# Two products held behind the weight split, and another order for the first transfers, in a hybrid recurrent and attention block

## The chip, the cores and the metric

The kernel runs on one core of a Trainium2 chip. The metric is the device time of one execution in microseconds (us); less is better. A profiled execution has a time of its own, and its trace gives start and length of every instruction on TensorE (PE), VectorE (DVE), ScalarE (ACT), GpSimd (POOL) and the queue of SyncE (SP), which issues all transfers here.

## The reference, cut to what matters

One layer of a residual block, in fp32, on one sequence of 512 positions with 2048 features:

```python
mod = silu(c) @ ada_w + ada_b             # six vectors of 2048: shift and scale (here SH1, SC1), gates, ...
h   = rms_norm(x) * (1 + scale) + shift   # adaLN modulation
p   = h @ w_in                            # recurrent x (1024) | recurrent y (1024) | 8 heads of q, k, v | forget logits
rec = rglru(conv4(p_x), gates) * gelu(p_y)            # width-4 causal convolution, then a scan along the positions
att = softmax(rms_norm(q) @ rms_norm(k).T + cum_logf) @ v   # 8 heads of 128, causal, 128-query blocks
x   = x + gate1 * (concat(rms_norm(rec), rms_norm(att)) @ w_out)
x   = x + gate2 * swiglu(modulate(rms_norm(x)))       # up projection, down projection
```

## The kernel before, in words

**Numbers.** Every fp32 product with a weight is made of three matmuls on rounded halves: both operands are split into a high part (an ACT copy to fp32r) and a low part (a DVE subtraction), and PE sums high x high, low x high and high x low. `wsplit` (L196) does this for a weight tile: whi on ACT, wlo on DVE. `tail_lo` is the list of the DVE subtractions issued so far, so `tail_lo[-1]` is the split of the newest weight tile at that place of the program.

**Stages in time.** Features lie on the 128 partitions, positions along a row (tiles of 128x512). From about 12 to 103 us `w1`: the first 1024 input columns, 16 steps (kt) of 24 matmuls into 8 PSUM banks. To 150 us `yr0`, from 150 to 185 us the first half of `h0`, to 503 us the heads `h1` to `h7`, each a projection (`tm_group`) into whose steps the attention of the head before, a pair of recurrent blocks, bias sums and adaLN products are hung as hooks. Then `yr1`, the output projection, the up projection and the down projection.

**The step of w1.** Before x is normed, the scale A of a feature must be known. For each kt `ada_fast(SC1, kt)` (L151) loads two 128x1024 tiles of the adaLN weight, `ada` and `adf`, and DVE multiplies each with silu(c), kept on all partitions in `c_b` and summed along the row (L159). L340 and L342 make A of the two sums, of `bg` (1 + a slice of `vec`, the table of all small vectors) and of a column of `vec`. ACT writes hph = x·A rounded (L345), DVE hpl (L346); ACT and DVE split the weights w1r into w1h and w1l (L352, L353); ACT squares x for the norm (L288). `c_b` comes of the input row `crow`: half is broadcast by a transfer, half by PE (cps), and ACT applies silu to both. `SH1` products run the same way under `yr0`, followed by `make_h`: x·A·rstd_x (L382), hh and hl (L384, L385), where rstd_x is the norm's factor, made at about 105 to 110 us.

**Attention and recurrence in the heads.** `attention()` gives a list of steps: `stats` (squares, sums, POOL's power), `norm` (L487: q and k times their factor), `qk_t` (transposes), `score` (L515 on PE, then on DVE the negated row maximum nm, L520, and later bt scaled by its sum, L524), `pt_` (transposes pt on PE, evacuated by ACT to pT, L534) and `pv` (L542 on PE into po). `rec_pair()` gives the recurrent steps: `fetch`, `conv` (L623: xrl times rstd_x on DVE, then the bias on ACT, L624, and the taps), `gates`, the scan. `ada_some` issues products of the other adaLN vectors (L149), always behind `tail_lo[-1]`; `bias_in` (L601) sums what the shift adds to the projections; `forget` makes the cumulative log-forget sums, which go to DRAM as `ct` and come back as `cb`.

**What sets the order.** The program is traced in source order and then scheduled per engine by priority. `tc.high_priority(offset)` moves an instruction forward; `with tc.issue_after(ins)` keeps what is issued inside it behind `ins` on the engine. Each engine then runs its list strictly in that order. All transfers go out on SP's queue in SP's order.

Of the kernel before, what the change touches and what calls it, by code (L numbers as in the profile page):

```python
# [8 lines left out]
F32 = mybir.dt.float32  # L9
F32R = mybir.dt.float32r  # L10
AF = mybir.ActivationFunctionType
ALU = mybir.AluOpType
AX = mybir.AxisListType

P = 128
D = 2048
S = 512
KT = D // P
NT = S // P
# [12 lines left out]
SH1, SC1, GT1, SH2, SC2, GT2 = range(6)  # L32
V_BADA, V_GMIX, V_GFFN = 0, 96, 112
# [24 lines left out]
def R(ap):  # L58
    return ap.bitcast(F32R)
# [3 lines left out]
def block_kernel(ctx, tc, xT, crow, adaT, vecs, bfr, w1, wyr, wqkv0, wqkv, wgate, wout, wup0, wups, wdown, outT):  # L63
    nc = tc.nc
# [3 lines left out]
    ap_ = ctx.enter_context(tc.tile_pool(name="ap", bufs=2))  # L68
# [8 lines left out]
    def page(name, tag, shape=None):  # L77
        return pgp.tile(shape or [P, S], F32, tag=tag, name=name, bufs=TAGS[tag])

    def acc(name):  # L80
        return psa.tile([P, S], F32, tag="acc", name=name)
# [10 lines left out]
    c_b = cp.tile([P, D], F32, name="c_b")  # L92
    vec = cp.tile([P, NVEC], F32, name="vec")
    with tc.high_priority(offset=100000):
        cr = wp.tile([P, 2048], F32, tag="raw", name="cr", bufs=RAW)
        nc.sync.dma_start(out=cr[:1, 1024:2048], in_=crow[:, 1024:2048])
        nc.sync.dma_start(out=c_b[:, :1024], in_=crow[:, :1024].broadcast_to([P, 1024]))
        one = cp.tile([P, P], F32, name="ones")
        nc.vector.memset(one, 1.0)
        nc.scalar.activation(c_b[:, :1024], c_b[:, :1024], AF.Silu)  # L100
        for q in (2, 3):
            cs = slice(q * 512, (q + 1) * 512)
            pc = acc(f"cps{q}")
            nc.tensor.matmul(pc, lhsT=one[:1, :], rhs=cr[:1, cs], start=True, stop=True)
            nc.scalar.activation(c_b[:, cs], pc, AF.Silu)
        nc.sync.dma_start(out=vec, in_=vecs)

    ident = cp.tile([P, P], F32, name="ident")
    make_identity(nc, ident)
# [17 lines left out]
    def vcol(base, i=0):  # L127
        return vec[:, base + i:base + i + 1]
# [22 lines left out]
    def ada_fast(j, i):  # L151
        for hf in range(2):
            cs = slice(hf * 1024, (hf + 1) * 1024)
            if hf:
                t = pgp.tile([P, 1024], F32, tag="qk", name=f"adf{j}_{i}", bufs=2)
            else:
                t = ap_.tile([P, 1024], F32, tag="ada", name=f"ada{j}_{i}")
            nc.sync.dma_start(out=t, in_=adaT[j * KT + i, :, cs])
            nc.vector.scalar_tensor_tensor(out=t, in0=t, scalar=1.0, in1=c_b[:, cs],  # L159
                                           op0=ALU.mult, op1=ALU.mult, accum_out=ada_acc[j][:, hf, i:i + 1])  # L160

# [6 lines left out]
    tail_lo = []  # L168
# [34 lines left out]
    def mm(ps, l, r, start, stop):  # L203
        nc.tensor.matmul(ps, lhsT=R(l), rhs=R(r), start=start, stop=stop)  # L204
# [76 lines left out]
    def rstd_bcast(*a, **kw):  # L281
        sums, spread = rstd_parts(*a, **kw)
        sums()
        return spread()

    def square_acc(ssq, src, first, name, tag):
        if first:
            nc.scalar.activation(ssq, src, AF.Square)  # L288
        else:
            sq = page(name, tag)  # L290
            nc.scalar.activation(sq, src, AF.Square)
            nc.vector.tensor_add(ssq, ssq, sq)
# [16 lines left out]

    ssq_x = cp.tile([P, S], F32, name="ssq_x", tag="ssq", bufs=2)  # L310
    bg = cp.tile([P, KT], F32, name="bg")
    nc.vector.tensor_scalar_add(bg, vec[:, V_BADA + SC1 * KT:V_BADA + (SC1 + 1) * KT], 1.0)

    def load_x(kt, name):
        t = ap_.tile([P, S], F32, tag="x", name=f"{name}{kt}", bufs=2)
# [7 lines left out]
    def w1_loads(kt):  # L323
        ada_fast(SC1, kt)
        xt = page(f"x{kt}", "b")
        nc.sync.dma_start(out=xt, in_=xT[kt])
        xs.append(xt)
        raws = [page(f"w1r{kt}_{i}", "d") for i in range(2)]
        for i in range(2):
            nc.sync.dma_start(out=raws[i], in_=w1[kt][:, i * 512:(i + 1) * 512])  # L330
        return xt, raws

    for kt in range(KT):
        if kt < 2:
            with tc.high_priority(offset=90000):
                xt, raws = w1_loads(kt)
        else:
            xt, raws = w1_loads(kt)
        a = cp.tile([P, 1], F32, name=f"A{kt}")
        nc.vector.scalar_tensor_tensor(out=a, in0=ada_acc[SC1][:, 0, kt:kt + 1], scalar=ada_acc[SC1][:, 1, kt:kt + 1],  # L340
                                       in1=bg[:, kt:kt + 1], op0=ALU.add, op1=ALU.add)
        nc.vector.tensor_mul(a, a, vcol(V_GMIX, kt))  # L342
        A.append(a)
        h, l = page(f"hph{kt}", "h"), page(f"hpl{kt}", "h")
        nc.scalar.activation(R(h), xt, AF.Copy, scale=a)  # L345
        nc.vector.scalar_tensor_tensor(out=R(l), in0=xt, scalar=a, in1=h, op0=ALU.mult, op1=ALU.subtract)  # L346
        hp.append((h, l))
        wh = wp.tile([P, 1024], F32, tag="whi", name=f"w1h{kt}")
        wl = wp.tile([P, 1024], F32, tag="wlo", name=f"w1l{kt}")
        for i in range(2):  # L350
            cs = slice(i * 512, (i + 1) * 512)
            nc.scalar.activation(R(wh[:, cs]), raws[i], AF.Copy)  # L352
            nc.vector.tensor_sub(R(wl[:, cs]), raws[i], wh[:, cs])  # L353
        square_acc(ssq_x, xt, kt == 0, f"sqx{kt}", "c")
        for f in range(8):
            fs = slice(f * P, (f + 1) * P)
            mm(w1ps[f], wh[:, fs], h, kt == 0, False)
            mm(w1ps[f], wh[:, fs], l, False, False)
            mm(w1ps[f], wl[:, fs], h, False, kt == KT - 1)
    xr = [None] * 8  # L360
    for f in (4, 5, 6, 7, 0, 1, 2, 3):
        t = page(f"xr{f}", "c")
# [8 lines left out]
    rstd_x = rstd_bcast(ssq_x, D, "rstd_x", bank=acc)  # L371
# [16 lines left out]
    def sh1_block(kt):  # L388
        ada_fast(SH1, kt)
        make_h(kt)  # L390
# [7 lines left out]
    for f in range(4):  # L398
        t = page(f"yr{f}", "c")
# [72 lines left out]
    def attention(h, q, k, v):  # L472
# [11 lines left out]
        def norm():  # L484
            ss = st["ss"]
            for a, z in ((0, q), (1, k)):
                nc.vector.tensor_tensor(z, z, ss[:, 4 * a:4 * a + 4].unsqueeze(2).broadcast_to([P, NT, P]), ALU.mult)  # L487

        def qk_t():
            qkT = []  # L490
# [120 lines left out]
    def rec_pair(ns):  # L611
# [8 lines left out]

        def conv(n):
            x = X[n]
            nc.vector.tensor_mul(x, x, rstd_x)  # L623
            nc.scalar.activation(x, x, AF.Identity, bias=bin_[:, n:n + 1])  # L624
            u = page(f"u{n}", "c")
            nc.scalar.activation(u, x, AF.Identity, scale=vcol(V_CW, n * 4 + 3), bias=vcol(V_CB, n))
            for j in (1, 2, 3):
                nc.vector.scalar_tensor_tensor(out=u[:, j:], in0=x[:, :S - j], scalar=vcol(V_CW, n * 4 + 3 - j),
                                               in1=u[:, j:], op0=ALU.mult, op1=ALU.add)
            U[n] = u  # L630
# [195 lines left out]
    for g in range(4):  # L826
# [10 lines left out]
        for f in range(4):  # L837
            kt = g * 4 + f
            t = page(f"x1_{kt}", "c")
# [145 lines left out]
    for f in range(2 * STD, FT):  # L985
        ps = [bank(f + 1, b, f"uf{f}p{b}") for b in range(4)]
        m = {p: ps[b][:, h * HS:(h + 1) * HS] for p, (b, h) in where.items()}
        for c in range(2):
            for p, hi, lo in fast_chunk(f, c):
                for k in range(4):  # L990
                    th, tl = T[p][c * 4 + k]
                    ks = slice(k * P, (k + 1) * P)
                    for n, (w, x) in enumerate(((hi, th), (hi, tl), (lo, th))):
                        first, last = c + k + n == 0, c == 1 and k == 3 and n == 2
# [21 lines left out]
    for pi, part in enumerate(PARTS):  # L1016
# [7 lines left out]
        for g in range(4):  # L1024
# [17 lines left out]
            for f in range(4):  # L1042
                kt = g * 4 + f
# [6 lines left out]
                if not last:  # L1050
                    t = page(f"dnt{kt}", "d")
# [71 lines left out]
```

## Time and profile before

| | |
|---|---|
| three runs | 2128.67, 2127.71, 2125.3 us; median 2127.71 |
| the profiled execution | 2128.95 us |
| its span, first to last instruction | 2127.2 us |
| PE busy | 2090.5 us, 98% of the span |
| DVE busy | 1527.9 us, 72% |
| ACT busy | 858.5 us, 40% |

All rows of the trace below are of that one profiled execution. Its own time is 1.75 us above its span and 1.24 us above the median of the runs. The busy shares are averages over the whole span; stages differ, and a wait on PE counts only where nothing later absorbs it.

### The profile page before, as it was taken

The page shows a single profiled execution, that of the slowest core. Times are in us where ns is not written, and L with a number is a line of the kernel's source. Part 1 is how long each engine was busy: PE and PEld are TensorE (multiplying, and loading weights), DVE is VectorE, ACT ScalarE, POOL GpSimd, SP SyncE. Part 2 cuts the span into 40 slices and gives each one's busy share as a digit, 9 for nine tenths or more (in the row PEclk, how much of TensorE's full clock was granted, in tenths as well). Part 3 has the DMA queues.
Part 4 walks back from the last instruction along what each step waited for, and adds up shares of the span by engine and source line. Part 5 has one row for each costly group of instructions (what it writes and reads, how often), then busy time and mean ns, then how long its engine had stood idle before and what let it go on. Part 6 is the DMA issues. An engine that isn't in the chain of part 4 may idle for free.

```text
span 2127.2 us, 32243 instructions
## 1 busy us (share of the span) xinstructions
PE 2090.5 (98%) x12737; PEld 1898.3 (89%) x12737; DVE 1527.9 (72%) x2403; ACT 858.5 (40%) x1200; POOL 33.9 (2%) x37
## 2 busy tenths in 40 slices
PE   8999999999999998999999999999999999999999
PEld 6889898888788887999999999999999888888887
DVE  8999768886877889888888888888887343323332
ACT  4433447764432346444444444444443222221111
POOL 0000000000100000000000000000000000000000
PEclk9999999999999999999999999999999999999999
DMA  9989766667777622443443443444436984653442
GB/s 336 347 292 318 234 216 218 220 223 260 239 266 260 236 100 99 133 136 125 128 145 120 130 142 126 129 135 130 133 128 199 320 301 171 208 191 134 156 152 100
DMA packets 133016, 406.00 MB, mean 191 GB/s; under 512 B 14561, under 2 KB 19841, under 8 KB 123138
## 3 DMA queue, kind: packets, MB, share of 16 engines
q1 hardware_dynamic: 132866, 403.96, 56.1%
q8 instruction: 99, 1.62, 0.3%
q14 instruction: 51, 0.42, 0.1%
HBM read 361.15 MB, written 42.75 MB: 190 GB/s over the span
## 4 chain that ended last, share of the span: by engine, by line
PE 88%; DVE 7%; DMA 3%; issue 1%; POOL 1%; ACT 1%; SPq 0%; DVEq 0%; ACTq 0%
PE dn_0p L204 6%; PE dn_3p L204 6%; PE dn_2p L204 6%; PE dn_1p L204 6%; PE w1p L204 4%; PE yr1p L204 2%; PE up0p L204 2%; PE wo3p L204 2%; PE wo2p L204 2%; PE wo1p L204 2%; PE up1p L204 2%; PE yr0p L204 2%; PE wo0p L204 2%; PE h3p L204 2%; PE h2p L204 2%; PE h7p L204 2%
## 5 line engine op out<-in xcount | busy, mean ns | idle before, releaser
L149 DVE SCALAR_TENSOR_TENSOR ada<-ada,c_b 128x1024 f32<-128x1024 f32 x128 | 154.6, 1222 | 47.2 <-DMA ada<-in_adaT 46.8
L200 DVE TENSOR_TENSOR uq_0tl<-uq_0r,uq_0th 128x1024 fp32r<-128x1024 f32 x40 | 49.0, 1225 | 62.4 <-ACT uq_0th L199 62.4
L199 ACT ACTIVATE uq_0sh<-uq_0r 128x1024 fp32r<-128x1024 f32 x40 | 42.5, 1062 | 92.6 <-PE uf4p L995 3.8
L200 DVE TENSOR_TENSOR uq_0al<-uq_0r,uq_0ah 128x1024 fp32r<-128x1024 f32 x40 | 49.0, 1225 | 39.7 <-ACT uq_0ah L199 39.6
L199 ACT ACTIVATE uq_1sh<-uq_1rb 128x1024 fp32r<-128x1024 f32 x40 | 42.5, 1063 | 70.7 <-PE uf43p L995 2.4
L199 ACT ACTIVATE uq_0th<-uq_0r 128x1024 fp32r<-128x1024 f32 x40 | 42.4, 1061 | 70.6 <-DVE uq_0r L975 1.9
L199 ACT ACTIVATE uq_1th<-uq_1ra 128x1024 fp32r<-128x1024 f32 x40 | 42.4, 1061 | 68.1 <-PE uf10p L995 1.8
L199 ACT ACTIVATE uq_1ah<-uq_1ra 128x1024 fp32r<-128x1024 f32 x40 | 42.5, 1062 | 60.6 <-issue 59.1
L199 ACT ACTIVATE uq_0ah<-uq_0r 128x1024 fp32r<-128x1024 f32 x40 | 42.4, 1061 | 49.1 <-issue 46.7
L200 DVE TENSOR_TENSOR uq_1tl<-uq_1ra,uq_1th 128x1024 fp32r<-128x1024 f32 x40 | 49.0, 1226 | 10.4 <-ACT uq_1th L199 10.4
L204 PE MATMUL w1p<-hph,w1h 128*128 128x512 f32 x128 | 47.6, 400 | 6.1 <-ACT hph L345 6.1
L200 DVE TENSOR_TENSOR uq_0sl<-uq_0r,uq_0sh 128x1024 fp32r<-128x1024 f32 x40 | 49.1, 1226 | 5.1 <-ACT uq_0sh L199 1.4
L200 DVE TENSOR_TENSOR uq_1sl<-uq_1rb,uq_1sh 128x1024 fp32r<-128x1024 f32 x40 | 49.0, 1226 | 3.7 <-ACT uq_1sh L199 1.5
L204 PE MATMUL w1p<-hpl,w1h 128*128 128x512 f32 x128 | 51.0, 398 | 0.0
L204 PE MATMUL w1p<-hph,w1l 128*128 128x512 f32 x128 | 50.8, 396 | 0.0
L200 DVE TENSOR_TENSOR uq_1al<-uq_1ra,uq_1ah 128x1024 fp32r<-128x1024 f32 x40 | 48.7, 1217 | 0.2
L200 DVE TENSOR_TENSOR dn_1l<-dn_2r,dn_1h 128x1024 fp32r<-128x1024 f32 x11 | 13.5, 1226 | 38.1 <-ACT dn_1h L199 38.1
L159 DVE SCALAR_TENSOR_TENSOR ada<-ada,c_b 128x1024 f32<-128x1024 f32 x32 | 39.1, 1222 | 2.3 <-DMA ada<-in_adaT 2.3
L200 DVE TENSOR_TENSOR dn_0l<-dn_2r,dn_0h 128x1024 fp32r<-128x1024 f32 x11 | 13.5, 1225 | 37.6 <-ACT dn_0h L199 37.6
L200 DVE TENSOR_TENSOR dn_1l<-dn_0r,dn_1h 128x1024 fp32r<-128x1024 f32 x11 | 13.5, 1225 | 37.4 <-ACT dn_1h L199 37.4
L200 DVE TENSOR_TENSOR dn_0l<-dn_3r,dn_0h 128x1024 fp32r<-128x1024 f32 x10 | 12.3, 1225 | 38.0 <-ACT dn_0h L199 38.0
L159 DVE SCALAR_TENSOR_TENSOR adf<-adf,c_b 128x1024 f32<-128x1024 f32 x32 | 39.1, 1222 | 0.1
(13786 smaller groups left out, 8152.5 us busy)
## 6 DMA issues: line engine op xcount, KB each, us to landing
ada<-in_adaT SPq DMA_DIRECT2D x160, 512.0 KB, 5.3
uq_0r<-in_wups SPq DMA_DIRECT2D x80, 512.0 KB, 4.3
uq_1ra<-in_wups SPq DMA_DIRECT2D x40, 512.0 KB, 4.0
uq_1rb<-in_wups SPq DMA_DIRECT2D x40, 512.0 KB, 3.2
adf<-in_adaT SPq DMA_DIRECT2D x32, 512.0 KB, 5.9
actd<-ach SPq DMA_DIRECT2D x44, 256.0 KB, 2.0
actd<-acl SPq DMA_DIRECT2D x44, 256.0 KB, 4.0
dn_0r<-in_wdown SPq DMA_DIRECT2D x11, 1024.0 KB, 4.9
```

What stands on the lines that cost most here:

```text
L149: nc.vector.scalar_tensor_tensor(out=t, in0=t, scalar=1.0, in1=cs, op0=ALU.mult, op1=ALU.mult, accum_out=ac)
L159: nc.vector.scalar_tensor_tensor(out=t, in0=t, scalar=1.0, in1=c_b[:, cs], op0=ALU.mult, op1=ALU.mult, accum_out=ada_acc[j][:, hf, i:i + 1])
L199: nc.scalar.activation(R(hi[:, :n]), raw_ap, AF.Copy)
L200: tail_lo.append(nc.vector.tensor_sub(R(lo[:, :n]), raw_ap, hi[:, :n]).ins)
L204: nc.tensor.matmul(ps, lhsT=R(l), rhs=R(r), start=start, stop=stop)
```

## The change

It has three parts. The first tile of the adaLN weight is loaded by the first transfer of the program, ahead of the row c. The table `vec` is loaded behind the first x tile instead of ahead of everything but c, and `bg`, which is computed from it, is issued with the first step of w1. The products of `norm` and the rescaling in `conv` are put behind the newest weight split on DVE.

```diff
     with tc.high_priority(offset=100000):
+        ada_first = ap_.tile([P, 1024], F32, tag="ada", name=f"ada{SC1}_0")
+        nc.sync.dma_start(out=ada_first, in_=adaT[SC1 * KT, :, :1024])
         cr = wp.tile([P, 2048], F32, tag="raw", name="cr", bufs=RAW)
         nc.sync.dma_start(out=cr[:1, 1024:2048], in_=crow[:, 1024:2048])
         nc.sync.dma_start(out=c_b[:, :1024], in_=crow[:, :1024].broadcast_to([P, 1024]))
...
             nc.scalar.activation(c_b[:, cs], pc, AF.Silu)
-        nc.sync.dma_start(out=vec, in_=vecs)
...
             else:
-                t = ap_.tile([P, 1024], F32, tag="ada", name=f"ada{j}_{i}")
-            nc.sync.dma_start(out=t, in_=adaT[j * KT + i, :, cs])
+                first = j == SC1 and i == 0
+                t = ada_first if first else ap_.tile([P, 1024], F32, tag="ada", name=f"ada{j}_{i}")
+            if hf or not first:
+                nc.sync.dma_start(out=t, in_=adaT[j * KT + i, :, cs])
...
     bg = cp.tile([P, KT], F32, name="bg")
-    nc.vector.tensor_scalar_add(bg, vec[:, V_BADA + SC1 * KT:V_BADA + (SC1 + 1) * KT], 1.0)
...
         nc.sync.dma_start(out=xt, in_=xT[kt])
         xs.append(xt)
+        if kt == 0:
+            nc.sync.dma_start(out=vec, in_=vecs)
...
             xt, raws = w1_loads(kt)
+        if kt == 0:
+            with tc.high_priority(offset=90000):
+                nc.vector.tensor_scalar_add(bg, vec[:, V_BADA + SC1 * KT:V_BADA + (SC1 + 1) * KT], 1.0)
...
             for a, z in ((0, q), (1, k)):
-                nc.vector.tensor_tensor(z, z, ss[:, 4 * a:4 * a + 4].unsqueeze(2).broadcast_to([P, NT, P]), ALU.mult)
+                with tc.issue_after(tail_lo[-1]):
+                    nc.vector.tensor_tensor(z, z, ss[:, 4 * a:4 * a + 4].unsqueeze(2).broadcast_to([P, NT, P]), ALU.mult)
...
             x = X[n]
-            nc.vector.tensor_mul(x, x, rstd_x)
+            with tc.issue_after(tail_lo[-1]):
+                nc.vector.tensor_mul(x, x, rstd_x)
```

The lists of the engines move at three places. First, DVE's list at the start of the program; ada_0 and adf_0 are the two adaLN tiles of kt 0, ada_1 and adf_1 those of kt 1, w1r_0 and w1r_1 the two halves of a step's weights; spn rows belong to a vector that is needed much later. Before:

```order
L312 TENSOR_SCALAR bg<-vec 128x16
L459 TENSOR_SCALAR gqs<-vec 128x1
L571 TENSOR_SCALAR zl<-vec 128x8
L159 SCALAR_TENSOR_TENSOR ada_0_136,ada_acc_114<-ada_0_136,c_b 128x1024
L159 SCALAR_TENSOR_TENSOR adf_0_139,ada_acc_114<-adf_0_139,c_b 128x1024
L300 TENSOR_SCALAR spns<-spne 128x8
L340 SCALAR_TENSOR_TENSOR A_148<-ada_acc_114,bg 128x1
L301 RECIPROCAL spns<-spns 128x8
L342 TENSOR_TENSOR A_148<-A_148,vec 128x1
```

The same place with the change:

```order
L162 SCALAR_TENSOR_TENSOR ada_0_80,ada_acc_115<-ada_0_80,c_b 128x1024
L345 TENSOR_SCALAR bg<-vec 128x16
L162 SCALAR_TENSOR_TENSOR adf_0_137,ada_acc_115<-adf_0_137,c_b 128x1024
L360 TENSOR_TENSOR w1l_156<-w1r_0_143,w1h_155 128x512
L347 SCALAR_TENSOR_TENSOR A_148<-ada_acc_115,bg 128x1
L360 TENSOR_TENSOR w1l_156<-w1r_1_144,w1h_155 128x512
L162 SCALAR_TENSOR_TENSOR ada_1_186,ada_acc_115<-ada_1_186,c_b 128x1024
L349 TENSOR_TENSOR A_148<-A_148,vec 128x1
```

Before, the second step of A stands in front of both splits w1l and of ada_1; now it stands behind them. On ACT the second weight copy w1h now also stands ahead of hph.

Second, DVE's list at the end of w1, where xr is the evacuation of w1's banks, sh a column of the shift, and the product with rstd_x the first step of `make_h`. Before:

```order
L159 SCALAR_TENSOR_TENSOR ada_1_1061,ada_acc_113<-ada_1_1061,c_b 128x1024
L364 COPY xr_978<-w1p_135 128x512
L364 COPY xr_986<-w1p_129 128x512
L364 COPY xr_994<-w1p_131 128x512
L266 COPY rstd_xt<-rstd_xa 128x4
L200 TENSOR_TENSOR yr_0l<-yr0r_1115,yr_0h 128x1024
L159 SCALAR_TENSOR_TENSOR adf_1_1064,ada_acc_113<-adf_1_1064,c_b 128x1024
L382 SCALAR_TENSOR_TENSOR x_142<-x_142,A_148,rstd_x 128x512
```

With the change:

```order
L371 COPY xr_994<-w1p_131 128x512
L269 COPY rstd_xt<-rstd_xa 128x4
L203 TENSOR_TENSOR yr_0l<-yr0r_1115,yr_0h 128x1024
L385 SCALAR_TENSOR_TENSOR sh_0_1042<-ada_acc_114,vec 128x1
L162 SCALAR_TENSOR_TENSOR ada_1_1061,ada_acc_114<-ada_1_1061,c_b 128x1024
L389 SCALAR_TENSOR_TENSOR x_140<-x_140,A_148,rstd_x 128x512
L162 SCALAR_TENSOR_TENSOR adf_1_1064,ada_acc_114<-adf_1_1064,c_b 128x1024
```

The product adf_1 went from ahead of the first x·A·rstd_x to behind it.

Third, the heads. ACT's list at the end of the projection h5, where pT_2 and pT_3 are evacuations of `pt_`, h_1h a weight split, and xrl<-xrl,bin the bias of `conv`. Before:

```order
L199 ACTIVATE h_1h<-h6r_4006 128x768
L534 ACTIVATE pT_2_3933<-pt_2_3930 128x256
L624 ACTIVATE xrl_4028<-xrl_4028,bin 128x512
L534 ACTIVATE pT_3_3960<-pt_3_3958 128x128
L468 ACTIVATE qk_3983<-h5p_3539 128x256
```

With the change:

```order
L202 ACTIVATE h_1h<-h6r_4006 128x768
L542 ACTIVATE pT_2_3933<-pt_2_3930 128x256
L542 ACTIVATE pT_3_3960<-pt_3_3958 128x128
L475 ACTIVATE qk_3983<-h5p_3539 128x256
L476 ACTIVATE v_3984<-h5p_3539 128x128
```

The bias of `conv` is gone from between the two evacuations; it stands in the next head. On DVE, at the start of the projection h5, in the attention of head 4 (sq, ss: its squares and sums; ada_11 a product of `ada_some`). Before:

```order
L200 TENSOR_TENSOR h_0l<-h5r_3653,h_0h 128x768
L149 SCALAR_TENSOR_TENSOR ada_11_0_3605,ada_acc_115<-ada_11_0_3605,c_b 128x1024
L292 TENSOR_TENSOR ssq_att<-ssq_att,sqa_3515 128x512
L480 TENSOR_REDUCE ss_3530<-sq_0_3531 128x4
L480 TENSOR_REDUCE ss_3530<-sq_1_3534 128x4
L149 SCALAR_TENSOR_TENSOR ada_11_1_3606,ada_acc_115<-ada_11_1_3606,c_b 128x1024
L487 TENSOR_TENSOR qk_3520<-qk_3520,ss_3530 128x4x128
```

With the change:

```order
L203 TENSOR_TENSOR h_0l<-h5r_3653,h_0h 128x768
L632 TENSOR_TENSOR xrl_3565<-xrl_3565,rstd_x 128x512
L295 TENSOR_TENSOR ssq_att<-ssq_att,sqa_3515 128x512
L487 TENSOR_REDUCE ss_3530<-sq_0_3531 128x4
L487 TENSOR_REDUCE ss_3530<-sq_1_3534 128x4
L150 SCALAR_TENSOR_TENSOR ada_11_0_3605,ada_acc_116<-ada_11_0_3605,c_b 128x1024
L495 TENSOR_TENSOR qk_3520<-qk_3520,ss_3530 128x4x128 x2
```

The first product of ada_11 now stands behind the two sums, and the rescaling of `conv` ahead of them. PE's list is the same from the third head on, POOL's everywhere.

## Rows read from the trace of the kernel before

**Rows 1.** The profile page: busy time of each engine over the span.

```profile
PE 2090.5 (98%) x12737; PEld 1898.3 (89%) x12737; DVE 1527.9 (72%) x2403; ACT 858.5 (40%) x1200; POOL 33.9 (2%) x37
```

**Rows 2.** Waits of PE by what ended them: us in total, times, longest.

```profile
PE s L515 <- DVE nm L520: 6.2, 4, 2.9
PE w1p L204 <- ACT hph L345: 6.1, 1, 6.1
...
PE po L542 <- ACT pT L534: 1.9, 1, 1.9
...
PE pt L530 <- DVE bt L524: 1.1, 2, 0.8
PE h0p L204 <- ACT hh L384: 1.0, 1, 1.0
...
PE s L515 <- ACT qkT L497: 0.6, 1, 0.6
```

**Rows 3.** Stretches: length, busy PE, PEld, DVE, ACT, POOL, PE clock, DMA share, GB/s.

```profile
20.00:100.00 80.00, 80.00 (x355) 66.24 (x354) 75.30 (x148) 34.73 (x58) 0.00 (x0) 1.00 0.95 349
120.00:180.00 60.00, 60.00 (x302) 54.82 (x302) 59.89 (x102) 18.98 (x24) 0.00 (x0) 1.00 0.93 320
226.60:230.00 3.40, 3.40 (x11) 2.73 (x10) 2.89 (x12) 2.37 (x10) 0.00 (x0) 0.50 0.73 274
```

**Rows 4.** Timeline of ACT, the start: start us, length us, instruction, idle before and its releaser.

```profile
10.21 0.63 ACT L288 ACTIVATE ssq_x<-x 128x512 f32<-128x512 f32 x1 [1.29 <-DMA x<-in_xT]
10.89 0.63 ACT L352 ACTIVATE w1h<-w1r 128x512 fp32r<-128x512 f32 x1
11.42 0.71 ACT L345 ACTIVATE hph<-x,A 128x512 fp32r<-128x512 f32 x1
```

**Rows 5.** Timeline of DVE, the start.

```profile
11.14 0.16 DVE L342 TENSOR_TENSOR A<-A,vec 128x1 f32<-128x1 f32 x1
11.94 0.69 DVE L353 TENSOR_TENSOR w1l<-w1r,w1h 128x512 fp32r<-128x512 f32 x1
...
13.88 1.22 DVE L159 SCALAR_TENSOR_TENSOR ada<-ada,c_b 128x1024 f32<-128x1024 f32 x1
```

**Rows 6.** Timeline of PE: the first matmuls of w1.

```profile
12.18 1.22 PE L204 MATMUL w1p<-hph,w1h 128*128 128x512 f32 x2 [6.11 <-ACT hph L345]
...
17.85 0.63 PE L204 MATMUL w1p<-hph,w1h 128*128 128x512 f32 x1
18.28 0.44 PE L204 MATMUL w1p<-hpl,w1h 128*128 128x512 f32 x1
```

**Rows 7.** Timeline of SP's queue: the first issue.

```profile
0.79 0.35 SPq L96 DMA_DIRECT2D cr<-in_crow  x1
```

**Rows 8.** Timeline of DVE, where rstd_x becomes ready.

```profile
106.43 1.22 DVE L159 SCALAR_TENSOR_TENSOR adf<-adf,c_b 128x1024 f32<-128x1024 f32 x1
...
110.42 0.75 DVE L382 SCALAR_TENSOR_TENSOR x<-x,A,rstd_x 128x512 f32<-128x512 f32 x1 [2.76 <-ACT rstd_x L277]
```

**Rows 9.** The chain that ended last, seen in head 0: start us, us, what.

```profile
215.50 2.79 DMA cum_d<-ct
...
218.35 6.87 DMA cb<-cum_d
```

**Rows 10.** Timeline of DVE in the projection h5.

```profile
368.07 1.23 DVE L149 SCALAR_TENSOR_TENSOR ada<-ada,c_b 128x1024 f32<-128x1024 f32 x1 [1.70 <-DMA ada<-in_adaT]
...
374.04 0.69 DVE L487 TENSOR_TENSOR qk<-qk,ss 128x512 f32<-128x512 f32 x1 [1.80 <-POOL ss L253]
```

**Rows 11.** Timeline of PE: the two later waits of score.

```profile
393.62 1.13 PE L515 MATMUL s<-qkT,qkT 128*128 128x512 f32 x2 [1.74 <-DVE nm L520]
...
441.03 1.12 PE L515 MATMUL s<-qkT,qkT 128*128 128x512 f32 x2 [1.25 <-DVE nm L520]
```

**Rows 12.** Timeline of ACT at the end of the projection h5.

```profile
411.40 0.72 ACT L624 ACTIVATE xrl<-xrl,bin 128x512 f32<-128x512 f32 x1 [4.68 <-DVE xrl L623]
```

**Rows 13.** Waits of DVE: us in total, times, longest.

```profile
DVE ada L149 <- DMA ada<-in_adaT: 46.8, 29, 3.7
```

## The prediction, made before the changed kernel ran

> **What bounds the kernel now.** I read the page first: PE is busy in 98% of the span, DVE in 72%, ACT in 40% [rows 1]. A change that removes no matmul can therefore only move PE's idle time, so the next view is the list of PE's waits [rows 2]. It names the waits near the places that the change touches: 6.1 us in one piece before the first matmul of w1, which ACT's hph ends; 6.2 us in four pieces in which a score waits for the row maximum of DVE; 1.9 us in one piece for an evacuation in a head; and some of 1 us or less. Then the stretches: in w1, between 20 and 100 us, PE is busy 80.00 of 80 us and DVE 75.30; between 120 and 180 us PE 60.00 of 60 and DVE 59.89 [rows 3]. So in w1 PE sets the pace with DVE close behind, and under yr0 both are full. Such a stretch gives nothing back: what is lost ahead of it stays lost. The rest of the working is in the timelines of the start and of the heads.
>
> **The start.** Before the change the order is x lands (its square starts at 10.21 on ACT), the first weight half is copied at 10.89, hph runs from 11.42 for 0.71 [rows 4], behind A's second step at 11.14, 0.16 long [rows 5], and PE's first matmul starts at 12.18 [rows 6]. Both w1l subtractions and ada_1 come later on DVE and cost PE nothing.
>
> With the change A's second step stands behind bg, adf_0, both w1l and ada_1, and hph behind the second w1h. I follow the slower engine at each point. The first w1h can start when its weights are there, by 10.89. ssq_x and the second w1h follow, at the 0.53 at which ACT's row of 10.89 is followed by the next: the second w1h is done at about 12.6. DVE then subtracts w1l in 0.69: 13.3. ada_1 takes 1.22: 14.5. A's second step 0.16, hph 0.71: 15.4, and PE starts at 15.45, 3.3 late. If ada_1 lands no earlier than the 13.88 at which its product starts today [rows 5], the chain is 13.88 + 1.22 + 0.16 + 0.71 = 15.97, with the same 0.05 to the matmul 16.0: 3.85 late. As x is one issue nearer the front (vec went behind it; an issue takes at least 0.35 [rows 7]), all could be 0.35 earlier: 3.0. The DVE side alone, bg waiting for vec behind x, then adf_0 1.22 and the first w1l, reaches the second w1l at about 12.7 too, so vec's new place adds nothing to the chain. I take 3.5, in the middle of 3.0 to 3.85. The earlier first tile of ada buys nothing: adf_0, x and the weights, which are later, decide.
>
> Does it stay lost? PE is busy in all of 20 to 100 us, so **+3.5**. One thing could give a part back. The first matmuls start 0.43 apart (17.85 to 18.28 [rows 6]), the 1.2 GHz level; in the long stretch 355 take 80 us, 0.225 each [rows 3], the 2.4 GHz level. Between 12.18 and 17.85 there are 14 at the slow pace. If the clock rises at 18.28 whatever PE did, a start at 15.7 has some 8 fewer slow matmuls, and the delay shrinks by 8 x 0.2 = 1.6. If it rises some time after matmuls begin, the slow part moves along and all 3.5 stand. The trace has a single rise here, and before it PE had been idle; I take the second.
>
> On this the Trainium skill, page "TensorE: Matmul & The Clock Gate", section "Part 1: The HAM clock gate", says that the throttled clock is the default state and that activity of the matmuls releases it. By that the sum keeps 3.5; by a rise at a fixed time it would be 1.9. The one rise in this trace, behind 14 slow matmuls, agrees with it and can't exclude the other.
>
> **The end of w1.** One product of 1.22, adf_1, goes from ahead of x·A·rstd_x to behind it. Today it runs at 106.43, and DVE then still idles 2.76 until rstd_x is there [rows 8], so it was free; now its 1.15 (1.22 less the overlap of successive rows) is added to a DVE that is full to 180 us [rows 3]. At the end of that stretch PE waits 1.0 for hh in h0p [rows 2], so the lag appears there: **+1.15**, from 0 (if the products' transfers leave DVE slack that the busy share hides) to 1.15. A wait of 2.1 is near the 2.9 behind which the clock stood at 0.50 for 3.4 us [rows 2, 3]; if it fell here as well, 3.4 x 0.5 = 1.7 more.
>
> **Head 0.** The longest score wait, 2.9 [rows 2], ends a chain: DVE's ct, its way to DRAM (2.79) and back as cb (6.87) [rows 9]. DVE's list has two more ba sums ahead of ct than before (128x512, as w1l 0.69 with a pitch of some 0.6), so ct is some 1.3 later, and three short matmuls more stand ahead of PE's wait, worth 0.5: **+1.0** when rounded up for the queue of transfers that cb stands in. Bounds 0 (a transfer that waited anyway) and 2.0.
>
> **The heads.** Here the change takes waits away. ACT's conv bias waited 4.68 for DVE's rescaling at the end of h5 and held the last evacuation pT behind it [rows 12]; PE lost 1.9 for po [rows 2]. With the rescaling behind a weight split the bias no longer stands between the evacuations: −1.9. In h5's attention DVE waited 1.70 for the transfer of an ada tile ahead of the two sums, so that the norm's product came at 374.04 behind a further wait for POOL [rows 10]; now the sums stand ahead of that product, and what the wait and the product cost (1.70 + 1.2) no longer delays them. The scores there lose 1.74 [rows 11] and 0.6 for qkT [rows 2]: both go. Of the four score waits, 6.2 − 2.9 − 1.74 − 1.25 leaves 0.3 for the smallest, which goes too, and the 0.8 before a pt [rows 2] with it. That is 1.9 + 1.7 + 0.6 + 0.3 + 0.8 = 5.3. In the next head a rescaling is added ahead of the scores, 0.6, and the wait of 1.25 there [rows 11] grows by it. Net **−4.7**. The gain is bounded by 5.3, if the growth is hidden, and by 1.3 if only the evacuation's 1.9 comes back and the 0.6 is paid.
>
> Nothing else changes: PE's list is the same from the third head on, and DVE's behind h7.
>
> **Sum.** 3.5 + 1.15 + 1.0 − 4.7 = +0.95 for a profiled execution: 2128.95 + 0.95 = 2129.9. The median of the runs shown is 1.24 lower than the profiled one, so the median forecast is 2128.7. A measurement tells about 0.2%, 4.3 us, from no change; the forecast lies within it.
>
> **Rivals.**
> *DVE in the heads goes at the pace of the ada transfers (slower).* DVE waits 46.8 us in 29 pieces for ada tiles [rows 13]. A product moved behind the sums may only meet the same transfer elsewhere: in h6 a product is put behind the scores, in h5 ahead of the norm, and each wait that was removed comes back at the next score. Then nothing of the 5.3 is got back, and the time is 3.5 + 1.15 + 1.0 + 0.6 = +6.25, 2134.0 in the median. It decides for slower when less than 2.0 of the 5.3 comes back (6.25 − 4.3). For it speaks the 46.8; against it that the longest, 1.9 for po, hangs on ACT's order and on no transfer.
> *The start is not lost (faster).* If the transfers, all a slot earlier or shorter in line, let ada_1 and the weights land well before 10.89, or DVE's order at run time costs PE nothing since w1h ends earlier, the 3.5 goes: −2.55, 2125.2. If the lags of 1.15 and 1.0 are hidden as well, it is −4.7, 2123.0, faster. Against it: the chain is of DVE's and ACT's own lengths, 0.69, 1.22, 0.16, 0.71, which no transfer shortens, and DMA is busy 0.95 in the stretch that follows [rows 3].
> *The clock rises at its own time.* −1.6 of the sum: −0.65, 2127.1.
> *The clock falls at the end of yr0.* +1.7: +2.65, 2130.4.
>
> **How the numbers follow.** The forecast has 0.45, with its own range from 2126 to 2131.5 (start 3.0 to 3.85, lags 0 to 3.15, heads −5.3 to −1.3, not all at one end). The pace of the transfers has 0.16, nearly all slower. The start not lost has 0.20, two thirds of it with the lags hidden and so faster. The clock by itself 0.08 and the fall 0.10, nearly all within 0.2%; 0.01 is left. So faster 0.15, same 0.66, slower 0.19. The range takes in both rivals' nearer halves: 2123.4 to 2133.2.
>
> **What would show it.** The first matmul of w1 at 15.2 to 16.0, behind hph behind A's second step behind ada_1: right; at 12.5 or before: the start's term is wrong. PE's wait for hh at h0p of about 2.1, and the clock behind it. The first score wait of head 0 at 3.5 to 4.5. No wait for po in h5 and none of 1.7 for nm there; a wait for nm of 1.8 in h6. If PE's waits in the heads add to as much as before, with DVE's waits for ada at 46.8 or more, the transfers set the pace and the prediction fails to the slow side; if w1 ends at the same time as before in spite of a later start, PE was not its bound.

## The result, and the profile after

The changed kernel is slower by a little: 2132.63 us in the median of 14 runs (2130.16 to 2136.7) against 2128.66 of the kernel before in 14 runs (2122.66 to 2130.97), ratio 1.0023, 95% interval 1.0015 to 1.0030. That is 3.2 to 6.4 us. The forecast was 2128.7, no change that can be told; the range, to 2133.2, holds the time.

The profiled execution spans 2129.7 us. Busy times on its page have not moved (PE 2091.2 us, DVE 1528.0, ACT 858.4; [rows 1]), as was expected of a change without new work. So the time is in PE's waits, the view that answers to [rows 2]:

```profile
PE w1p L207 <- ACT hph L352: 8.4, 1, 8.4
PE s L523 <- DVE nm L528: 3.9, 3, 2.9
...
PE h5p L207 <- ACT v L476: 2.3, 1, 2.3
PE h0p L207 <- ACT hh L391: 2.2, 1, 2.2
...
PE h6p L207 <- ACT v L476: 1.8, 1, 1.8
```

The wait for po is gone and the score waits have fallen from 6.2 to 3.9, as forecast. But two waits for v, the evacuation of a head's projection, have come up: 2.3 at the start of h5 (0.7 before) and 1.8 at the start of h6 (none before).

Sums of waits don't tell what is made up later. The table below does: how much later (+) or earlier (−) the same matmul starts than in the kernel before, at eight places, from the traces of both kernels, median of the matmuls around the place. Places are named by their time in the kernel before. All runs of the experiments are in it.

```
                     first  yr0    h1     h3     h5     h5     heads' up     
                     12 us  130    190    300    372    408    end 500  815
after                +3.75  +2.23  +4.94  +5.13  +7.86  +5.07  +4.31  +4.81
e1 hold alone        -0.06  -0.68  -0.68  -1.62  +1.27  -1.56  -1.12  -1.00
e2 start alone       +4.06  +3.24  +5.68  +6.98  +9.44  +7.59  +6.86  +6.92
e3 ada first only    +3.57  +2.54  +5.15  +5.76  +8.13  +6.65  +6.75  +6.78
e4 vec late only     +1.75  +1.22  +3.64  +4.07  +7.20  +5.77  +4.92  +4.95
e5 hold, copy ahead  -0.62  -0.05  -0.04  -0.24  -0.38  -2.12  -5.00  -4.62
e6 after, copy ahead +4.35  +2.75  +5.47  +5.75  +4.76  +2.79  -1.06  -0.95
e7 hold, no loads    -0.44  -1.41  -1.41  -0.40  -1.89  -2.51  -5.95  -4.79
e8 product back      +3.03  +0.20  +2.71  +3.81  +3.90  +1.60  +1.66  +2.22
e9 copy ahead alone  -1.18  -2.19  -2.21  -0.29  -1.48  -1.85  -4.95  -4.12
```

The row "after" reads: 3.75 late at the first matmul, of which 1.5 is given back by yr0, most of it through the clock; 2.7 lost at the end of yr0; nothing gained from there to the end of the heads but 0.6. Behind 815 us the profiled execution of the kernel before has a bad stretch (its clock is 0.85 from 824 to 858 us, 0.90 in the changed kernel, and no list differs there), which shortens the gap of the two spans to 2.4; the medians, 4.0 apart, and the ratio don't share it.

**The start.** ACT's timeline of the changed kernel, which answers to [rows 4]:

```profile
8.51 1.06 ACT L102 ACTIVATE c_b<-c_b 128x1024 f32<-128x1024 f32 x1 [6.45 <-DMA c_b<-in_crow]
...
11.51 0.63 ACT L359 ACTIVATE w1h<-w1r 128x512 fp32r<-128x512 f32 x1 [0.57 <-DMA w1r<-in_w]
...
12.57 0.61 ACT L359 ACTIVATE w1h<-w1r 128x512 fp32r<-128x512 f32 x1
15.15 0.72 ACT L352 ACTIVATE hph<-x,A 128x512 fp32r<-128x512 f32 x1 [1.97 <-DVE A L349]
```

And DVE's, which answers to [rows 5]:

```profile
9.60 1.23 DVE L162 SCALAR_TENSOR_TENSOR ada<-ada,c_b 128x1024 f32<-128x1024 f32 x1 [8.55 <-ACT c_b L102]
...
13.21 0.69 DVE L360 TENSOR_TENSOR w1l<-w1r,w1h 128x512 fp32r<-128x512 f32 x1 [0.22 <-ACT w1h L359]
13.82 1.22 DVE L162 SCALAR_TENSOR_TENSOR ada<-ada,c_b 128x1024 f32<-128x1024 f32 x1
...
14.97 0.15 DVE L349 TENSOR_TENSOR A<-A,vec 128x1 f32<-128x1 f32 x1
```

The chain is the forecast one: second w1h, w1l, ada_1, A's second step, hph. It is some 0.5 later than the sum's 15.45, since the first w1h waits for its weights until 11.51, where the sum has 10.89. The first matmul comes at 15.93 instead of 12.18. The reader also sees what the forecast did not follow: c now lands behind the 512 KB tile, so silu(c) begins at 8.51, and the first product, which has its tile, waits for c. In the kernel before it began 3.15 earlier:

```profile
5.36 1.06 ACT L100 ACTIVATE c_b<-c_b 128x1024 f32<-128x1024 f32 x1 [0.37 <-DMA c_b<-in_crow]
```

PE's timeline there, which answers to [rows 6]:

```profile
15.93 1.65 PE L207 MATMUL w1p<-hph,w1h 128*128 128x512 f32 x3 [8.41 <-ACT hph L352]
...
19.51 0.46 PE L207 MATMUL w1p<-hph,w1l 128*128 128x512 f32 x1
19.81 0.40 PE L207 MATMUL w1p<-hph,w1h 128*128 128x512 f32 x1
```

Starts are 0.43 apart to 19.51, but for a first step of 0.59, and some 0.23 from 19.81 on. The slow part is 15.93 to 19.51 here, 8 steps, and 12.18 to 18.28 in [rows 6], 13 steps. Five slow steps fewer, at 0.43 instead of 0.23, give back 1.0. The second and third step of the kernel before took 0.65 and 0.59 and take 0.43 here, which gives back 0.4 more. So 3.75 becomes 2.4, the lag in the middle of w1.

**The end of yr0.** DVE's timeline, first and last product with rstd_x, which answers to [rows 8]:

```profile
112.87 0.75 DVE L389 SCALAR_TENSOR_TENSOR x<-x,A,rstd_x 128x512 f32<-128x512 f32 x1 [2.76 <-ACT rstd_x L280]
...
184.09 0.94 DVE L203 TENSOR_TENSOR h_1l<-h1r,h_1h 128x768 fp32r<-128x768 f32 x1
184.96 0.20 DVE L385 SCALAR_TENSOR_TENSOR sh<-ada_acc,vec 128x1 f32<-128x1 f32 x1
185.09 0.73 DVE L389 SCALAR_TENSOR_TENSOR x<-x,A,rstd_x 128x512 f32<-128x512 f32 x1
```

and ACT's hh behind it, for which PE waits:

```profile
185.86 0.72 ACT L391 ACTIVATE hh<-x,sh 128x512 fp32r<-128x512 f32 x1 [2.67 <-DVE x L389]
```

From the first of these products to hh it is 72.99 us. In the kernel before the same end is

```profile
180.55 0.75 DVE L382 SCALAR_TENSOR_TENSOR x<-x,A,rstd_x 128x512 f32<-128x512 f32 x1
181.21 0.95 DVE L200 TENSOR_TENSOR h_1l<-h1r,h_1h 128x768 fp32r<-128x768 f32 x1
182.08 0.21 DVE L378 SCALAR_TENSOR_TENSOR sh<-ada_acc,vec 128x1 f32<-128x1 f32 x1
```

```profile
182.32 0.72 ACT L384 ACTIVATE hh<-x,sh 128x512 fp32r<-128x512 f32 x1 [1.36 <-DVE sh L378]
```

and hh comes 71.90 behind the first product, at 110.42 [rows 8]. DVE is full there, so its list is its time. The split h_1l of the next head's weights (0.87) and the column sh went from behind the last product to ahead of it, but hh needs sh as well and stood behind all three in either kernel. New ahead of hh is adf_1 alone, 1.15, and hh comes 1.09 later for it. PE waits 2.22 for hh and then runs slowly:

```profile
186.63 0.48 PE L207 MATMUL h0p<-h_1h,hh 128*128 128x392 f32 x1 [2.22 <-ACT hh L391]
186.91 0.53 PE L207 MATMUL h0p<-h_1l,hh 128*128 128x392 f32 x1
187.24 0.53 PE L207 MATMUL h0p<-h_1h,hh 128*128 128x392 f32 x1
```

0.33 from start to start against 0.18 ahead of the wait. The wait grew by 1.27: the 1.09, and 0.2 because the first product with rstd_x is 2.45 later than before and PE in yr0 only 2.23. The slow stretch cost 1.4 more: together the 2.7 of the table.

**The start of h5.** Here the gain of the heads went. PE:

```profile
370.81 0.44 PE L207 MATMUL h5p<-h_0h,hh 128*128 128x384 f32 x1 [2.34 <-ACT v L476]
```

ACT, a step back along the chain:

```profile
370.48 0.45 ACT L476 ACTIVATE v<-h4p 128x128 f32<-128x128 f32 x2 [3.29 <-DVE qk L473]
```

DVE, a further step back; the last row is the copy of q and k that ACT waits for:

```profile
364.29 1.23 DVE L150 SCALAR_TENSOR_TENSOR ada<-ada,c_b 128x1024 f32<-128x1024 f32 x1 [1.58 <-DMA ada<-in_adaT]
...
366.59 1.23 DVE L150 SCALAR_TENSOR_TENSOR ada<-ada,c_b 128x1024 f32<-128x1024 f32 x1 [0.20 <-DMA ada<-in_adaT]
...
368.88 1.23 DVE L150 SCALAR_TENSOR_TENSOR ada<-ada,c_b 128x1024 f32<-128x1024 f32 x1 [1.05 <-DMA ada<-in_adaT]
...
370.03 0.75 DVE L473 COPY qk<-h4p 128x256 f32<-128x256 f32 x2
```

And SP's queue, where the tile of 364.29 was issued:

```profile
354.93 0.33 SPq L213 DMA_DIRECT2D h5r<-in_wqkv  x1
...
357.74 0.33 SPq L139 DMA_DIRECT2D ada<-in_adaT  x1
```

PE waits for v, v for the copy of q and k, and that copy stands behind three adaLN products, each of which waits for a tile; the first tile was issued behind a weight tile of h5 and its product began 6.55 after its issue. In the kernel before a product with a late tile also stands ahead of this copy, and PE lost 0.7 there:

```profile
362.32 1.23 DVE L149 SCALAR_TENSOR_TENSOR ada<-ada,c_b 128x1024 f32<-128x1024 f32 x1 [0.74 <-DMA ada<-in_adaT]
...
363.47 0.75 DVE L466 COPY qk<-h4p 128x256 f32<-128x256 f32 x2
```

The copy is 6.56 later now, while PE was 4.94 late when it came there. The hold is not needed for that: e2, e3 and e4 below, which have none, wait 1.8 to 2.2 for v at this place. The waits of DVE for ada tiles, 46.8 in [rows 13], are 39.1 here in 29 pieces as before: fewer in sum, but 2.8 of them right ahead of this copy, against 1.6 (the 0.74 and one of 0.89). Only two buffers hold these tiles; those of 366.59 and 368.88 were issued at 362.07 and 365.55, right behind the end of an earlier product. Whether a third buffer would take the waits away was not tried. Behind both waits for v the clock falls, as the stretches show (columns as in [rows 3]; the clock is the number behind POOL's):

```profile
370.80:374.00 3.20, 3.19 (x10) 3.06 (x11) 2.31 (x4) 3.17 (x8) 0.00 (x0) 0.56 0.93 326
418.90:422.00 3.10, 3.10 (x8) 2.00 (x8) 2.76 (x5) 3.05 (x7) 0.00 (x0) 0.52 0.57 210
```

### The profile page after: what moved, and what is told of

It is laid out like the page before. It is cut to its first block, busy times and chain, and to the rows that moved or that the text cites. A ratio compares the mean times of both kernels' runs of the same rounds, so it can differ in the third digit from the quotient of the medians.

```text
span 2129.7 us, 32233 instructions
## 1 busy us (share of the span) xinstructions
PE 2091.2 (98%) x12737; PEld 1899.4 (89%) x12737; DVE 1528.0 (72%) x2403; ACT 858.4 (40%) x1200; POOL 33.6 (2%) x37
## 3 DMA queue, kind: packets, MB, share of 16 engines
q8 instruction: 99, 1.62, 0.3%
## 4 chain that ended last, share of the span: by engine, by line
PE 87%; DVE 8%; DMA 2%; issue 1%; ACT 1%; POOL 1%; SPq 0%; DVEq 0%; ACTq 0%
PE dn_0p L207 6%; PE dn_3p L207 6%; PE dn_1p L207 6%; PE dn_2p L207 6%; PE w1p L207 4%; PE yr1p L207 2%; PE up0p L207 2%; PE wo3p L207 2%; PE wo2p L207 2%; PE wo1p L207 2%; PE yr0p L207 2%; PE wo0p L207 2%; PE h3p L207 2%; PE h2p L207 2%; PE h7p L207 2%
## 5 line engine op out<-in xcount | busy, mean ns | idle before, releaser
L150 DVE SCALAR_TENSOR_TENSOR ada<-ada,c_b 128x1024 f32<-128x1024 f32 x128 | 154.2, 1220 | 39.5 <-DMA ada<-in_adaT 39.1
L202 ACT ACTIVATE uq_0ah<-uq_0r 128x1024 fp32r<-128x1024 f32 x40 | 42.4, 1060 | 49.2 <-issue 46.8
L203 DVE TENSOR_TENSOR dn_1l<-dn_2r,dn_1h 128x1024 fp32r<-128x1024 f32 x11 | 13.5, 1226 | 38.2 <-ACT dn_1h L202 38.2
L203 DVE TENSOR_TENSOR dn_0l<-dn_2r,dn_0h 128x1024 fp32r<-128x1024 f32 x11 | 13.5, 1225 | 37.6 <-ACT dn_0h L202 37.6
L203 DVE TENSOR_TENSOR dn_1l<-dn_0r,dn_1h 128x1024 fp32r<-128x1024 f32 x11 | 13.5, 1226 | 37.6 <-ACT dn_1h L202 37.6
L203 DVE TENSOR_TENSOR dn_0l<-dn_0r,dn_0h 128x1024 fp32r<-128x1024 f32 x11 | 13.5, 1226 | 37.0 <-ACT dn_0h L202 35.4
```

Of the source, the lines that this page charges most:

```text
L202: nc.scalar.activation(R(hi[:, :n]), raw_ap, AF.Copy)
L203: tail_lo.append(nc.vector.tensor_sub(R(lo[:, :n]), raw_ap, hi[:, :n]).ins)
```

## The experiments

In norm's products the hold moves nothing: with that edit alone the engines' lists are those of the kernel before, row for row, and from within h2 on the traces of e1 and of the changed kernel show the same lists. So "the hold" below is that of `conv`. It moves rows of DVE only from the projection h2 on, and the change of the start only ahead of that, so the two can be tried apart.

**e1, the hold alone.**

```diff
+            with tc.issue_after(tail_lo[-1]):
-            nc.vector.tensor_mul(x, x, rstd_x)
+                nc.vector.tensor_mul(x, x, rstd_x)
```

> The start as before; only the rescaling of conv is held behind the newest weight split (the hold on norm's products, tried by itself in the lists, moves no instruction, so it has no run). Theory A, the hold only trades waits: the wait for po (1.9) and the long score waits (1.74) go, but waits for v's evacuation behind DVE's qk copy come at the starts of h5 and h6 (2 us each), because products behind late ada transfers stand ahead of that copy; sum of PE's lag at the end of the heads between -1 and +1 us, time within 0.1% of before. Theory B, the hold does what was forecast and only the shifted start spoils it: no new wait for v, lag -4 to -5 us at the end of the heads, time about 2124.

Measured: 2125.51 against 2127.57, ratio 0.9990 (0.9981 to 0.9999). Its waits:

```profile
PE s L515 <- DVE nm L520: 4.3, 3, 2.0
...
PE h5p L204 <- ACT v L469: 2.4, 1, 2.4
...
PE h6p L204 <- ACT v L469: 1.5, 1, 1.5
```

With the start of before, both waits for v come all the same. The one at h6 is the hold's: no kernel without it (before, e2, e3, e4, e9) waits there, and the three that have it, with the products and their transfers in the old place, wait 1.5 to 2.6 (e1, the changed one, e8). The one at h5 is not shown to be the hold's. In e1 DVE's copy runs when it ran before, at 363.34 for 363.47, and PE, 1.8 ahead of the kernel before by then, waits 1.7 longer:

```profile
363.34 0.75 DVE L466 COPY qk<-h4p 128x256 f32<-128x256 f32 x2
```

In the table the lead is 1.62 at h3 and 1.12 at the end of the heads: the heads give nothing. The 1.6 was there ahead of the hold's first moved row, so it is of this execution and not of the edit. Theory A's signs are all there, with that doubt on the first wait; B, −4 to −5, falls. The ratio's 0.1% can be the hold's or not; its interval all but reaches 1.

**e2, the start alone** (both edits of the start, no holds).

> The two changes of the start without the holds. Theory A: first matmul at 15.9, PE 2.0 to 2.7 us late at the end of w1, a wait for hh of 2.2 at the end of yr0 with the clock falling behind it, so 4.5 to 5 us late in the heads, and the same at the end: 2132 to 2133.5. Theory B has the same here. A rival, that the heads absorb a late start: lag back under 2 us by the end of the heads, time within 0.1% of before.

Measured: 2133.13, ratio 1.0026 (1.0016 to 1.0036), as slow as the whole change. First matmul 16.24, wait for hh 2.2:

```profile
PE s L522 <- DVE nm L527: 6.1, 4, 3.8
...
PE h0p L207 <- ACT hh L391: 2.2, 1, 2.2
...
PE h5p L207 <- ACT v L476: 1.9, 1, 1.9
```

PE is 5.7 late at h1 and 6.9 at the end of the heads, a little more than either theory said; the score wait of head 0 is 3.8 here, and 2.9 in the whole change, whose list is the same there. The heads absorb nothing of a late start. The expectation did not have the last row: the late start alone makes PE wait for v at h5, 1.9 here and 1.8 and 2.2 in e3 and e4, against 0.7 before; none of the three waits at h6.

**e3, only the first ada tile ahead of c.**

```diff
+        nc.sync.dma_start(out=ada_first, in_=adaT[SC1 * KT, :, :1024])
         cr = wp.tile([P, 2048], F32, tag="raw", name="cr", bufs=RAW)
```

> Only the first ada tile ahead of c; vec stays ahead of the other tiles, bg early, no holds. If c behind the tile of 512 KB is the cause of the late start, c_b's first half is there at about 8.5 instead of 5.4 and the first matmul comes at 14.3 to 15 (A's second step now stands ahead of ada_1, 1.2 less than 15.9). If vec's place is the cause, the first matmul is at 12 to 12.6. At the end of yr0 the moved product is there too, so a wait for hh near 2 in both.

Measured: 2134.48, ratio 1.0034 (1.0021 to 1.0046), first matmul at 15.75, later than expected. ACT's timeline says why:

```profile
8.73 1.06 ACT L102 ACTIVATE c_b<-c_b 128x1024 f32<-128x1024 f32 x1 [6.66 <-DMA c_b<-in_crow]
...
13.58 1.28 ACT L303 ACT_TABLE_LOAD   x1
...
14.99 0.71 ACT L349 ACTIVATE hph<-x,A 128x512 fp32r<-128x512 f32 x1
```

c is late as expected (8.73), and A's second step ends at 14.26, but a table load for the spn rows had come to stand ahead of hph. With it taken off, 14.99 would be some 14.3 and the matmul at about 15.05, the end of the expected 14.3 to 15.

**e4, only vec behind the first x tile.**

```diff
         xs.append(xt)
+        if kt == 0:
+            nc.sync.dma_start(out=vec, in_=vecs)
```

> Only vec behind the first x tile with bg in the first step; c first, no holds. If c behind the ada tile is the cause of the late start, c_b is there at 5 to 5.4 and the first matmul at 12 to 13.5; if vec's place is the cause, at 14.5 to 16. The product at the end of w1 is moved here too: a wait for hh near 2 at the end of yr0 and PE about 2 us late in the heads, or more where the clock falls.

Measured: 2132.71, ratio 1.0026 (1.0017 to 1.0035), first matmul at 13.93, a little behind the expected 13.5. ACT:

```profile
5.59 1.06 ACT L100 ACTIVATE c_b<-c_b 128x1024 f32<-128x1024 f32 x1 [0.61 <-DMA c_b<-in_crow]
...
12.66 0.70 ACT L348 ACTIVATE hph<-x,A 128x512 fp32r<-128x512 f32 x1
```

With c first, c is on time, and A is ready at 11.3 as before; hph stands behind the same table load (11.25 to 12.53), and w1h behind hph. So each half of the start's change makes the first matmul late: e3 by 3.6, chiefly through c; e4 by 1.75, through the order on ACT. Both move adf_1, both have a wait for hh of 2.2, and both lose 2.4 to 2.6 between yr0 and h1.

**e5, the hold, and the copy of q and k ahead of the products.** The block of adaLN products of step 13 is issued behind the copy instead:

```diff
-H_ADA = (1, 4, 7, 10, 13)
+H_ADA = (1, 4, 7, 10)
...
-                nc.vector.tensor_copy(out=qk[:, t, :], in_=ps[t][:, 0:256])
+                evac_ins.append(nc.vector.tensor_copy(out=qk[:, t, :], in_=ps[t][:, 0:256]).ins)
...
             ev = head_evac(h, ps)
+        if h >= 3:
+            with tc.issue_after(evac_ins[-1]):
+                ada_some(1)
```

> As e1 (start as before, conv's rescaling held), and of the five adaLN products blocks of a head the one of step 13 is issued behind the DVE copy of q and k instead, so that no product stands between the last weight split of a head and that copy; the work is the same. If the new waits for v (2.43 at h5, 1.50 at h6 in e1) come from products with late transfers ahead of that copy, both fall under 0.6 and PE is 3.5 to 5 us ahead of the kernel before at the end of the heads, against 1.1 in e1: median near 2122. If it is the load of DVE as such, or the transfers of the products move the wait on to the scores, waits for nm or bt of 1.5 or more come in their place and the lead stays under 2 us.

Measured: 2123.35 against 2128.32, ratio 0.9976 (0.9968 to 0.9985): faster than the kernel before by 5 us in the medians. No wait for v above 0.25 is left. DVE at the start of h5:

```profile
359.34 0.96 DVE L200 TENSOR_TENSOR h_1l<-h5r,h_1h 128x768 fp32r<-128x768 f32 x1
362.26 0.42 DVE L468 COPY qk<-h4p 128x256 f32<-128x256 f32 x1 [1.96 <-PE h4p L204]
```

The copy now waits for PE's last matmul and for nothing else. The lead grows from 0.24 at h3 to 5.00 at the end of the heads. One score wait of h4 has grown from 0.3 to 1.8, so a part of the rival came too.

**e6, the same edit on the changed kernel.**

> The changed kernel with the same edit as e5. If the waits for v (2.34 and 1.80, and the clock at half behind each) are what ate the holds' gain, they fall under 0.6 and PE's lag on the kernel before is 0.5 to 2 us at the end of the heads instead of 4.3: median about 2129.5. If not, the lag stays at 3.5 to 5: median 2132 to 2133.

Measured: 2127.57 against 2128.32, ratio 0.9999 (0.9990 to 1.0008). The waits for v are gone; from 5.75 late at h3 PE comes to 1.06 early at the end of the heads, more than expected. So with the products behind the copy the heads give 4.8 (e5) to 6.8 us, and ahead of it next to nothing.

**e7, the hold, without transfers of the products.** As e1, but the products of the four later adaLN vectors read a tile that is already there (`in0=cs`), and their transfers are left out, so these vectors are not the reference's.

> As e1, but the products of the four later adaLN vectors read a tile that is there already, and their 64 transfers of 1 MB are left out, so these four vectors are not those of the reference. DVE's list keeps the products, at the same length. If late transfers cause the waits for v, both are gone (under 0.4) and no wait of more than 1 is left in h4 to h7. If the length of DVE's work causes them, the waits for v stay over 1.2.

One run, 2123.49. The waits for v are gone with the same products on DVE, so late tiles made them, not the length of DVE's work. A wait for po of 1.3 and a score wait of 1.7 are left in h5 and h6, against the expectation. With 64 MB less to move, the weights come sooner as well, so this run alone would not tell the tiles from the queue; e5, in which all transfers stay, does.

**e8, the changed kernel with the product back ahead.**

```diff
-        ada_fast(SH1, kt)
+        if kt == 1:
+            with tc.high_priority(offset=150):
+                ada_fast(SH1, kt)
+        else:
+            ada_fast(SH1, kt)
```

> The changed kernel with the products of the second SH1 step at a higher priority, so that four products stand ahead of the first x times rstd_x again. If the moved product causes the longer wait at the end of yr0, the wait for hh falls from 2.2 to about 1.0 and PE is some 2 us less late in head 1 (2.7 to 3.5 instead of 4.9), and the median falls to 2130 to 2131. If the late start as such causes it, the wait stays at 2.2 and the time at 2132 to 2133.

Measured: 2130.26 against 2128.32, ratio 1.0014 (1.0004 to 1.0023), and the two signs disagree: the wait for hh is still 2.2, but PE is 2.71 late at h1, as expected of the product's return. The rows of DVE settle it:

```profile
113.12 1.42 DVE L389 SCALAR_TENSOR_TENSOR x<-x,A,rstd_x 128x512 f32<-128x512 f32 x2 [0.21 <-ACT rstd_x L280]
...
183.11 0.78 DVE L389 SCALAR_TENSOR_TENSOR x<-x,A,rstd_x 128x512 f32<-128x512 f32 x1
```

The idle 2.76 ahead of the first row is used up to 0.21 (adf_1 and a split yr_1l stand in it now), and the last row comes at 183.11 instead of 185.09: 69.99 from first to last, 2.2 less than in the changed kernel, and hh is 1.6 later than before instead of 3.5. But PE also comes 2 earlier (0.20 late in yr0), so its wait is as long. The wait was the wrong sign to look for; the lag of hh was the right one. In time e8 and the changed kernel are not told apart (the intervals overlap).

**e9, the copy ahead of the products, without the hold.**

> The kernel before with only the edit of e5: one block of products of each head behind the DVE copy of q and k, conv's rescaling not held. If the hold and the products' place are two gains that need each other (the hold frees the scores and po, the place keeps v's evacuation free), the wait for po of about 1.9 stays here and the time is 1 to 3 us under before: 2125 to 2127.5. If the place is the whole gain of e5, po's wait goes too and the time is 2122.5 to 2124. If it is nothing without the hold: within 1 us of before.

Measured: 2124.83 against 2127.28, ratio 0.9992 (0.9981 to 1.0002), not told from no change. The expectation that po's wait stays is wrong: of the 1.9 in h5 nothing is left, and one of 0.5 stands in h4. In its trace the heads give 4.7 from h3 to their end, as in e5 (4.8). So by the traces the place of the products is the gain and the hold adds nothing to it that can be seen; by the times e5 is the better, and the intervals of the two overlap a little. That stays open.

## Why the prediction was wrong

**The start, +3.5.** The mechanism and its size at the first matmul hold: 3.75. Two things were off. "The earlier first tile of ada buys nothing" was right, but it also costs: c lands 3.15 later (3.4 in e3), and only because the chain over w1h and ada_1 is as long did that not show. And the clock did give back a part: five slow steps fewer, 1.0, and with 0.4 of longer steps 2.4 is left in w1. That is nearer the rival's 1.9 than the 3.5 that was taken, though the clock rose later than the rival's 18.28. (The forecast's 14 slow matmuls from 12.18 to 17.85 are 13 in the trace.) Over the eleven profiled kernels the slow steps were 7 to 13, with first matmuls from 11.00 to 16.53 and the end of the slow part between 14.91 and 21.52; neither a fixed time nor a fixed number describes it. On this the Trainium skill's page "TensorE: Matmul & The Clock Gate", section "Part 1: The HAM clock gate", has activity release the throttle; that the end moves between 14.91 and 21.52, on the whole with the start, agrees with it.

**The end of w1, +1.15.** The product's price was right, 1.09, and so was the wait, 2.1 forecast and 2.2 measured. The fall of the clock behind the wait, which the sum left out and gave a chance of 0.10 at a price of 1.7, came at 1.4. In all +2.7.

**Head 0, +1.0.** The wait was 2.9 as before, and PE's lag grew by 0.2 from h1 to h3 (4.94 to 5.13), next to the lower bound of 0; the sign, a first score wait of 3.5 to 4.5, did not show. In e2, with the same list there, the wait was 3.8 and the lag grew by 1.3, so the size of this wait varies from execution to execution.

**The heads, −4.7.** This is the step that failed. The waits that it named went: po's 1.9, the 1.74, the 0.6 for qkT, the 0.8 before pt. The 1.25 in h6, which was to grow to 1.8, fell to 0.5. But it asked only which waits would go, and put those that would come at 0.6: it did not ask where DVE would meet its next late tile. Products stand ahead of the copy of q and k, DVE waits for their tiles there, and PE waits for v: 1.6 more at h5, 1.8 at h6, and behind each the clock's fall, some 1.3 (PE is 4.94 late ahead of the first and 7.86 behind it, 2.92, of which 1.62 is the wait) and 1.5 (5.07 to 6.51 at the second, with 1.8 lost and po's 1.9 gained). From h3 to the end of the heads the change gave 0.8 (5.13 to 4.31), the hold alone cost 0.5 (1.62 to 1.12 early). It also took the heads' gain as the same whether the start is late or not, and the wait at h5 comes with the late start alone (e2 to e4). It is the first rival's mechanism, "it may only meet the same transfer elsewhere", at another place than the next score that it named, and its limit held: less than 2.0 of the 5.3 came back and the kernel is slower. Its signs did not show: PE's waits from h3 to the end of the heads are 5.1 us against 7.6 before (pieces over 0.25), and DVE waits 39.1 for ada tiles, not 46.8 or more. Taking the tiles' waits away from that copy gives 4.8 (e5) and 6.8 (e6), which shows the cause: the products ahead of the copy. That 4.8 is next to the forecast's 4.7 does not show that the hold was worth it, as e9 has 4.7 without the hold.

**Sum.** In place of 3.5 + 1.15 + 1.0 − 4.7 = +0.95 the trace has 2.2 to yr0, 2.7 at its end, 0.2 to h3 and −0.8 in the heads: +4.3, close to what the medians (4.0) and the ratio (4.9) say; single traces differ by up to 2 us, so a part of the agreement is luck.

## What to carry to other kernels

When a wait is taken out of an engine's strict list, ask what the freed work runs into next: follow the moved rows to the next late transfer, and look at who stands behind it there. A product that waits for a tile belongs behind the copy that empties the next PSUM banks, not ahead of it; that order and the hold together gave 0.24% here (e5), the order alone 0.08%, not told from no change (e9), and the hold alone gave nothing in the heads (e1). And of the first transfers, look at the one on which all first products depend, however small it is: a tile of 512 KB ahead of it made c 3.15 us later here.

## What the runs showed of the hardware that was not expected

The clock's fall behind a wait cost more than half as much as the wait itself: 1.4, 1.3 and 1.5 behind waits of 2.22, 2.34 and 1.80, with granted clocks of 0.56 and 0.52 in the stretches behind the latter two.

At the start of the kernel before, the view shows a granted clock of 1.00 while the matmuls start 0.43 apart [rows 6], the pace of the lower level:

```profile
12.20:18.30 6.10, 6.09 (x14) 4.30 (x15) 6.06 (x18) 2.45 (x5) 0.00 (x0) 1.00 1.01 380
```

The trace has no clock entry before 18.37 us, and the view counts what has none as 1.00. In all eleven profiles the first entry comes within 0.2 us of the place where the pace changes, so ahead of it only the pace tells the clock.

And one list does not give one time: with the lists of the kernel before up to head 0, the long score wait there was 2.9, 2.0, 2.8 and 3.6 (before, e1, e5, e9), with the changed start 2.9, 3.8 and 2.7 (after, e2, e6); and behind 815 us every profiled kernel made up 0.2 to 2.5 us against the one trace of the kernel before. Differences of 2 us between two profiled executions say nothing unless a row that the edit moved explains them.
